# Table steps in VectorE's gaps, retention's state in PSUM, and later column turns in a two-layer hybrid trunk

## The chip, the cores and the metric

The kernel runs on one core of a Trainium2 chip. The metric is the device time of one execution in microseconds (us); each kernel is run several times and the median counts.

## The reference

Two layers of `x <- x + W_out(concat[A(h) * silu(g_A), B(h) * silu(g_B)])` with `h = RMSNorm(x)`, then a last RMSNorm. There are 2048 tokens, 1024 channels, float32.

```
A: 8 heads x 64, softmax over the own chunk of 64 tokens and 8 chunks before it,
   scores * 64**-0.5 + rel_bias[h, clip(distance, -256, 256)]
B: 4 heads x 128, retention in chunks:
   q, k = rotary(q), rotary(k) * 128**-0.5
   o_intra = (q k^T * decay^|i-j|) v          inside a chunk
   o_inter = (q * q_decay) state              state of the chunks before
   state   = state * chunk_decay + (k * k_decay)^T v
   o = rms_norm(o_intra + o_inter)
```

## The kernel before

**Tiles.** Tokens lie in 16 tiles of 128 (`t`) and 4 supertiles of 512 (`n`). A layer is worked in 4 column groups `s`; each group holds two attention heads and one retention head. Per group and supertile, `dense_T` (L736; L719 for the very first) makes q and k for attention and for retention with channels on partitions, and `dense_V` (L755) makes v, the retention v and the gates with tokens on partitions. Every float32 product is made of three float16 products (upper times upper, and both cross terms), so each operand is split into an upper half (ScalarE) and a rest (VectorE). After the four groups `wout` (L1098) multiplies by W_out, adds to x and, in the first layer, makes the next layer's normed columns in `residual`.

**Who sets the order.** The orders on TensorE, ScalarE, VectorE and GpSimd are those in which the Python code issues; the planner leaves them alone. SP, which starts all DMAs, is ordered by hand in the first supertile alone; after that the planner orders its queue by its own estimates. The body is a sequence of rounds of 8 matmuls of 512 columns. `later(k, fn)` puts a step off by k rounds, `pull` brings in background steps (weights for the next group, norms, tables), and `attention` and `retention` of one supertile run under the dense products of the next.

**The first list.** Up to the first `dense_V`, the steps stand in one hand-written list of names that `do` runs in order: `xsq xrs xmul xtr xhi xlo` plus a digit are the steps of a tile's norm (square sum, inverse root, scaling, transposes, upper, rest), `Wsq Wlp Wsc Whi Wlo` and `V...` the steps of a weight section (square sum, cast, scale, upper, rest), `d` the next piece of the first `dense_T`, `t` and `u` the next step of the rotary tables of supertiles 0 and 1, `r` a step of the reversed bias, `g` of the gain, `bs` of the bias scratch, `Tu` and `Vu` the small factors. A table takes 17 steps: one on ScalarE, 13 on VectorE (L93 to L115), the sines on ScalarE (L117, L118), a copy (L120), and 8 stores that SP starts (L125 to L128). The cast in `Vlp2` (L1238) feeds a matmul of ones (L1244) that stands in TensorE's order between two pieces of `d`.

**Retention.** Per tile of 128 tokens, `retention` makes `r1` (the masked products, split into `dT`), then `r2` in PSUM: columns 0 to 127 the output, 128 to 255 the update of the state. One round later `add` (L897, L900 for the first tile) makes `state = update + state` in SBUF; then `upper_of` (L861, ScalarE) and `rest_of` (L865, VectorE) split it into `sh`, which the next tile's `r2` reads; at round 5 ScalarE multiplies the state by the decay in place (L905). `root` and `fin` (L914) finish the output from `r2`. `psR` holds the four PSUM buffers for these.

**Attention's output.** `pv` (L823 to L825) makes `o`; `out_` takes the reciprocal of the sum (L829), multiplies it by the scale `ka` (L830, two tensors of one column) and applies it (L835). The probabilities' rests are made on GpSimd (L813) and turned by a DMA transpose (`pT`).

**Border.** In `wout` of the first layer a tile takes 6 rounds. When its second half is done, SP stores it to `x_d` (L1107) and `residual` sets events at rounds after it: square sum at 2, root at 3. Tiles 5, 6, 7, 9, 10, 11 are turned by TensorE (`on_pe`: `mul` L994 at 5, `turn` L999 at 7, upper 8, rest 9); the others by two DMA transposes from row buffers (`mul` 4, upper 5, rest 6, `transpose_rows` L235, L236 at 7). Tiles 0 to 3 put these rows into slots 2 and 3 of the next layer's weight tiles, in turn. `y_turn` uses the same two lines for W_out's operands (`yhy`, `yly`).

Of the kernel before, what the change touches and what calls it, by code (L numbers as in the profile page):

```python
# [27 lines left out]
def hybrid_trunk(ctx: ExitStack, tc: tile.TileContext, x, pos, gain, gcol, w_in, w_out, rel, fgain,  # L28
# [569 lines left out]
    def later(k, fn):  # L598
        deferred.append([k, fn])
# [181 lines left out]
    def attention(l, s, n, g, st, prev):  # L781
        units = []
        for a in range(4):
            for hx in range(2):
                units.append((a, hx))
        ya = {}

        def qk(a, hx):

            u = St()  # L790
            u.a, u.hx = a, hx
            u.nm = f"{l}_{s}_{n}_{a}_{hx}"
            u.nb = nb = min(5, 4 * n + a + 1)
            u.w = w = nb * P
            u.kts = [(st if t // 4 == n else prev, t % 4) for t in range(4 * n + a + 1 - nb, 4 * n + a + 1)]
            S = psS.tile([P, 1024], F32, tag="S", name=f"S{u.nm}")
            cs = slice(a * P, (a + 1) * P)
            cuts = sorted({0, nb} | {j for j in range(nb) if u.kts[j] == (st, 0) or j == 4})
            for j0, j1 in zip(cuts, cuts[1:]):
                q_, a_ = u.kts[j0]  # L800
                k_ = q_.k[:, hx, a_ * P:(a_ + j1 - j0) * P]
                o = S[:, j0 * P:j1 * P]
                pe.matmul(o, st.q[:, hx, 0, cs], k_, start=True, stop=False)  # L803
                pe.matmul(o, st.q[:, hx, 1, cs], k_, start=False, stop=True)  # L804
            v = b2.tile([P, 640], F32, tag="sc", name=f"sc{u.nm}")[:, 0:w]
            m = b2.tile([P, 1], F32, tag="mq", name=f"mq{u.nm}")
            dve.tensor_tensor_reduce(out=v, in0=S[:, 0:w], in1=g.bias[hx][:, 640 - w:640], scale=1.0, scalar=-3.0e38,  # L807
                                     op0=ALU.add, op1=ALU.max, accum_out=m)
            dve.tensor_scalar(m, m, g.nc[:, 0:1], LN_PSC, op0=ALU.mult, op1=ALU.add)
            act.activation(v, v, AF.Exp, bias=m[:, 0:1], scale=g.c[:, 0:1])  # L810
            pq = b2.tile([P, 1280], F16, tag="pq", name=f"pq{u.nm}")
            act.activation(pq[:, 0:w], v, AF.Copy)  # L812
            pool.tensor_tensor(pq[:, w:2 * w], v, pq[:, 0:w], op=ALU.subtract)  # L813
            u.p = b2.tile([P, 10, P], F16, tag="pT", name=f"pT{u.nm}")[:, 0:2 * nb, :]
            later(1, lambda: sp.dma_start_transpose(out=u.p, in_=pq[:, 0:2 * w]))
            return u

        def pv(u):
            t = 4 * n + u.a
            o = psR.tile([P, 512], F32, tag="small", name=f"o{u.nm}")  # L820
            for b, (q_, a_) in enumerate(u.kts):
                v_ = q_.v[:, a_, u.hx, :]
                pe.matmul(o[:, 0:65], u.p[:, b, :], v_[:, 0:65], start=(b == 0), stop=False)  # L823
                pe.matmul(o[:, 0:64], u.p[:, b, :], v_[:, 65:129], start=False, stop=False)  # L824
                pe.matmul(o[:, 0:65], u.p[:, u.nb + b, :], v_[:, 0:65], start=False, stop=(b == u.nb - 1))  # L825

            def out_():
                rl = b2.tile([P, 1], F32, tag="rl", name=f"rl{u.nm}")
                dve.reciprocal(rl, o[:, 64:65])  # L829
                dve.tensor_tensor(rl, rl, g.ka, op=ALU.mult)  # L830
                if u.hx == 0:
                    ya[u.a] = b2.tile([P, P], F32, tag="ya", name=f"ya{u.nm}")
                y = ya[u.a]
                vs = slice(u.hx * 64, u.hx * 64 + 64)
                dve.scalar_tensor_tensor(out=y[:, vs], in0=o[:, 0:64], scalar=rl[:, 0:1], in1=st.g[u.a][:, vs],  # L835
                                         op0=ALU.mult, op1=ALU.mult)
                if u.hx == 1:
                    sp.dma_start(y_d[t][:, s * P:(s + 1) * P], y)

            later(1, out_)  # L840

        ret = retention(l, s, n, g, st)
        rounds_ret = (5, 10, 10, 14, 14, 18, 18, 23) if (l, s, n) == (0, 0, 0) else [6 * a + b for a in range(4) for b in (0, 5)]
        for i, (a, hx) in enumerate(units):
            flow(1)
            u = qk(a, hx)
            for r in range(3 * i, 3 * i + 3):
                for _ in range(rounds_ret.count(r)):
                    next(ret, None)
                if r % 3 == 2:  # L850
                    pipe.append(lambda u=u: pv(u))
                yield
# [14 lines left out]
    def retention(l, s, n, g, st):  # L867
        for a in range(4):
# [18 lines left out]
            if not last:  # L887
                kh, kl = st.kt[:, a, :], st.kt[:, 4 + a, :]
                products(r2[:, P:2 * P], [(kh, rv[:, 0]), (kh, rv[:, 1]), (kl, rv[:, 0])])
                if t == 0:  # L890
                    ring["state"] = b1.tile([P, P], F32, tag="state", name=f"state{nm}")
                ns = ring["state"]
                sh = ring["halves"] = b1.tile([P, 2, P], F16, tag="sh", name=f"sh{nm}")

                def add(r2=r2, ns=ns, t=t):
                    if t > 0:
                        dve.scalar_tensor_tensor(out=ns, in0=r2[:, P:2 * P], scalar=2.0 ** (-7 - s), in1=ns,  # L897
                                                 op0=ALU.mult, op1=ALU.add)
                    else:
                        dve.tensor_scalar(ns, r2[:, P:2 * P], 2.0 ** (-7 - s), None, op0=ALU.mult)  # L900

                later(1, add)
                later(2, lambda sh=sh, ns=ns: upper_of(sh, ns))
                later(3, lambda sh=sh, ns=ns: rest_of(sh, ns))
                later(5, lambda ns=ns: act.activation(ns, ns, AF.Copy, scale=(1.0 - 2.0 ** (-5 - s)) ** P))  # L905
            ss = b2.tile([P, 1], F32, tag="rss", name=f"rss{nm}")

            def root(ss=ss):
# [71 lines left out]
    def residual(l, t, xt, at, rows, on_pe):  # L980

        hh, hl = (h_[:, :, t % 4 * P:(t % 4 + 1) * P] for h_ in hT_of(l, t // 4))
        nm = f"n{l}_{t}"
        u = St()

        def sq():
            u.ss = squares(xt.rearrange("p (k c) -> p k c", c=P), nm, hh)

        def root():
            u.rs = rms_of(u.ss, gains[l].m, gains[l].e, nm)  # L990

        def mul():
            u.x = xt if on_pe or rows else psS.tile([P, D], F32, tag="S", name=f"xn{nm}")
            dve.scalar_tensor_tensor(out=u.x, in0=xt, scalar=u.rs[:, 0:1], in1=gains[l].b, op0=ALU.mult, op1=ALU.mult)  # L994

        def turn():
            u.p = psS.tile([P, KT, P], F32, tag="S", name=f"pt{nm}")
            for kt in range(KT):
                pe.transpose(u.p[:, kt, :], xt[:, kt * P:(kt + 1) * P], ident)  # L999

        def upper():
            if on_pe:
                act.activation(hh, u.p, AF.Copy)
            else:
                u.rows = rows or row_pair(nm)
                rows_hi(u.rows, u.x)

        def lower():
            if on_pe:
                dve.tensor_tensor(hl, u.p, hh, op=ALU.subtract)  # L1010
            else:
                rows_lo(u.rows, u.x)

        at(2, sq)
        at(3, root)
        if on_pe:
            at(5, mul)
            at(7, turn)
            at(8, upper)
            at(9, lower)  # L1020
        else:
            at(4, mul)
            at(5, upper)
            at(6, lower)
            at(7, lambda: transpose_rows(u.rows, hh, hl))

    def final_half(t, xt, c):

# [30 lines left out]
    def wout(l, go, gc, us, wT=None):  # L1059
# [6 lines left out]
        for r in range(6 * NT):  # L1066
# [32 lines left out]
            if i % 3 == 2:  # L1099
# [4 lines left out]
                if c == 1:  # L1104
                    at = lambda k, fn, r=r: events.setdefault(r + k, []).append(fn)
                    if not end:
                        sp.dma_start(x_d[t], u.x)  # L1107
                        rows = [w_[:, 2 + t % 2].rearrange("p k c -> p (k c)") for w_ in (wT.g.h, wT.g.l)]
                        residual(l + 1, t, u.x, at, rows if t < 4 else None, 4 < t < 12 and t % 4 > 0)
                    elif t + 1 < NT:  # L1110
                        final(t, u.x, at)
            yield
# [238 lines left out]
    def rounds(lists):  # L1351
# [1 line left out]
            do(names)  # L1353
            yield

    do("xsq0 g g xrs0 g Wsq0 Wlp0 Wsc0 xmul0 xtr0 Whi0 xsq1 xhi0 xrs1 xlo0 xmul1 Wlo0 xsq2 d t Wsq1 xrs2 xtr1 t xhi1 Wlp1 xmul2 "
# [3 lines left out]
    g00.vdone = 4  # L1360
    push(rounds(["xhi4 xrs5 xrs6", "xlo4 xmul5 xrs7", "xdma4 xhi5 xmul6 bt", "xlo5 xhi6", "xdma5 xlo6 xmul7", "xdma6 xhi7",
                 "xlo7", "xdma7 bt", "x8 u", "u x8 bt", "u u x8", "u u x8 bt"]), 12)
# [141 lines left out]
```

## Time and profile before

| What | us |
|---|---|
| median of 3 runs | 2089.33 |
| lowest, highest | 2085.60, 2089.53 |
| the profiled execution's own time | 2084.99 |
| its span, first to last instruction | 2083.2 |
| TensorE busy in it | 2008.0 |
| VectorE, ScalarE, GpSimd busy | 1245.1, 1141.9, 679.1 |

Busy times are of one execution, taken by the hardware profiler. PE is TensorE's matmuls, PEld its weight loads, DVE VectorE, ACT ScalarE, POOL GpSimd, SP the engine that starts DMAs. In a row of the timeline stand the start, the duration, engine and line, the operation, what it writes and reads, and in brackets how long the engine sat idle before it and what ended that. The granted clock is the share of full speed at which TensorE was let run.

### The profile page before, as it was taken

The numbers are of one execution on the slowest core, as the hardware profiler recorded it, in microseconds if no ns is written. First come the engines' busy times: TensorE is split into PE (matmuls) and PEld (weight loads), VectorE is DVE, ScalarE is ACT, GpSimd is POOL, SyncE is SP. The second block draws the span as 40 slices with busy tenths as digits, with TensorE's granted clock in tenths as the row PEclk, the third lists the DMA queues.
The fourth block names the chain that finished last, engine by engine and source line by source line (L and its number), as shares of the span: only waits on it lengthen the run. The fifth ranks groups of instructions, "written<-read, shape, count | busy, mean of one in ns | idle before, by whom it ended". The sixth has DMA issues, their size and how long they took to land.

```text
span 2083.2 us, 39398 instructions
## 1 busy us (share of the span) xinstructions
PE 2008.0 (96%) x14014; PEld 1051.6 (50%) x14014; DVE 1245.1 (60%) x3817; ACT 1141.9 (55%) x2530; POOL 679.1 (33%) x701
## 2 busy tenths in 40 slices
PE   6988999999999999998999999999999999999998
PEld 4444555555555555544444555555555555554543
DVE  7776666556556655676653656565655566557643
ACT  7556665456565654554444546554655665446432
POOL 0234343444344434330003343434243334333100
PEclk9999999999999999999999999999999999999999
DMA  8768675547575754799774547555655867548974
GB/s 233 166 152 172 143 164 106 117 112 158 114 185 118 158 141 102 158 227 259 200 188 98 124 102 147 119 124 102 142 119 125 182 145 166 122 102 192 213 197 126
DMA packets 645701, 313.63 MB, mean 151 GB/s; under 512 B 459232, under 2 KB 602080, under 8 KB 645504
## 3 DMA queue, kind: packets, MB, share of 16 engines
q1 hardware_dynamic: 645504, 311.12, 66.0%
q8 instruction: 109, 1.79, 0.4%
q14 instruction: 88, 0.72, 0.1%
HBM read 123.26 MB, written 41.98 MB: 79 GB/s over the span
## 4 chain that ended last, share of the span: by engine, by line
PE 48%; DMA 3%; POOL 1%; issue 1%; DVE 1%; ACT 1%; SPq 0%; POOLq 0%; ACTq 0%; DVEq 0%
PE dT L736 14%; PE dV L755 14%; PE dO L1098 13%; DMA pT<-pq 2%; PE r L857 2%; PE S L804 1%; PE S L803 1%; PE o L823 1%; PE o L824 1%; PE o L825 1%; DMA toep<-rel_d 0%; POOL pq L813 0%; PE ptn L999 0%; DMA stO1m<-in_w_out_dram 0%; ACT sc L810 0%
## 5 line engine op out<-in xcount | busy, mean ns | idle before, releaser
L813 POOL TENSOR_TENSOR pq<-sc,pq 128x640 f16<-128x640 f32 (+4 forms) x256 | 319.9, 1250 | 894.6 <-ACT pq L812 479.7
L810 ACT ACTIVATE sc<-sc,mq,cT 128x640 f32<-128x640 f32 (+4 forms) x256 | 218.5, 853 | 623.8 <-DVE rl L829 324.3
L736 PE MATMUL dT<-hTh,whT 128*128 128x512 f16 x1008 | 350.4, 383 | 5.0 <-DMA hTh<-xa 2.2
L755 PE MATMUL dV<-whV,hTh 128*128 128x512 f16 x1024 | 353.1, 381 | 1.7 <-DVE gt L773 1.3
L755 PE MATMUL dV<-wlV,hTh 128*128 128x512 f16 x1024 | 353.0, 380 | 0.0
L755 PE MATMUL dV<-whV,hTl 128*128 128x512 f16 x1024 | 352.8, 380 | 0.0
L736 PE MATMUL dT<-hTl,whT 128*128 128x512 f16 x1008 | 348.4, 381 | 0.0
L736 PE MATMUL dT<-hTh,wlT 128*128 128x512 f16 x1008 | 348.1, 380 | 0.0
L755 PEld LDWEIGHTS <-hTh 128*128 128x128 f16 x2048 | 196.5, 98 | 217.0 <-DVE gt L773 3.8
L736 PEld LDWEIGHTS <-whT 128*128 128x128 f16 x2016 | 193.1, 98 | 217.8 <-issue 12.9
L807 DVE CUSTOM_DVE_ANT_0 sc<-S,bias 128x640 f32<-128x640 f32 (+4 forms) x256 | 188.4, 736 | 125.3 <-PE S L804 124.6
L1098 PE MATMUL dO<-whO,yhy 128*128 128x512 f16 x512 | 194.6, 380 | 1.0 <-DMA yhy<-hTh 0.8
L1098 PE MATMUL dO<-whO,yly 128*128 128x512 f16 x512 | 194.3, 380 | 1.2 <-DMA yly<-hTl 0.6
L1098 PE MATMUL dO<-wlO,yhy 128*128 128x512 f16 x512 | 194.4, 380 | 0.0
L812 ACT ACTIVATE pq<-sc 128x640 f16<-128x640 f32 (+4 forms) x256 | 171.5, 670 | 8.1
L1098 PEld LDWEIGHTS <-yhy 128*128 128x128 f16 x1024 | 99.8, 98 | 116.1 <-DMA yhy<-hTh 1.3
L755 PEld LDWEIGHTS <-hTl 128*128 128x128 f16 x1024 | 99.2, 98 | 110.8 <-issue 1.7
L736 PEld LDWEIGHTS <-wlT 128*128 128x128 f16 x1008 | 97.5, 98 | 112.9 <-issue 6.2
L823 PE MATMUL o<-v,pT 128*128 128x65 f16 x1120 | 130.5, 194 | 15.6 <-DMA pT<-pq 15.5
L803 PE MATMUL S<-k,q 128*128 128x128 f16 (+3 forms) x592 | 143.6, 269 | 0.0
L823 PEld LDWEIGHTS <-pT 128*128 128x128 f16 x1120 | 106.0, 97 | 53.0 <-DMA pT<-pq 24.4
L804 PE MATMUL S<-k,q 128*128 128x128 f16 (+3 forms) x592 | 131.0, 269 | 0.0
(352 smaller groups left out, 3497.3 us busy)
## 6 DMA issues: line engine op xcount, KB each, us to landing
q<-qq SPq DMA_DIRECT2D x128, 128.0 KB, 2.5
yyy<-y_d SPq DMA_DIRECT2D x32, 512.0 KB, 4.9
stT<-in_w_in_dram SPq DMA_DIRECT2D x27, 512.0 KB, 5.0
stV<-in_w_in_dram SPq DMA_DIRECT2D x26, 512.0 KB, 4.5
k<-kk SPq DMA_DIRECT2D x128, 64.0 KB, 2.0
swp<-rot SPq DMA_DIRECT2D x64, 128.0 KB, 2.7
tabc<-tab SPq DMA_DIRECT2D x32, 256.0 KB, 2.7
tabs<-tab SPq DMA_DIRECT2D x32, 256.0 KB, 3.1
```

Of the source, the lines that this page charges most:

```text
L736: pe.matmul(ps, w_[:, j, kt, :], h_[:, kt, :], start=(m == 0), stop=(m == 23))
L755: pe.matmul(ps, h_[:, kt, a * P:(a + 1) * P], w_[:, kt, :], start=(m == 0), stop=(m == 23))
L803: pe.matmul(o, st.q[:, hx, 0, cs], k_, start=True, stop=False)
L804: pe.matmul(o, st.q[:, hx, 1, cs], k_, start=False, stop=True)
L807: dve.tensor_tensor_reduce(out=v, in0=S[:, 0:w], in1=g.bias[hx][:, 640 - w:640], scale=1.0, scalar=-3.0e38, op0=ALU.add, op1=ALU.max, accu ...
L810: act.activation(v, v, AF.Exp, bias=m[:, 0:1], scale=g.c[:, 0:1])
L812: act.activation(pq[:, 0:w], v, AF.Copy)
L813: pool.tensor_tensor(pq[:, w:2 * w], v, pq[:, 0:w], op=ALU.subtract)
L823: pe.matmul(o[:, 0:65], u.p[:, b, :], v_[:, 0:65], start=(b == 0), stop=False)
L824: pe.matmul(o[:, 0:64], u.p[:, b, :], v_[:, 65:129], start=False, stop=False)
L857: pe.matmul(out_, w_, m_, start=(i == 0), stop=(i + 1 == len(pairs)))
L1098: pe.matmul(ps, h_[:, kt, :], w_[:, kt, :], start=(m == 0), stop=(m == 23))
```

## The change

- The first list is ordered anew. The steps are the same; only their places differ. Four table steps stand right behind the norm of the third tile, the rests of a tile and of a weight swap places in places, and the last table steps stand further back.
- In retention, `add` writes the new state into columns 384 to 511 of `r2` in PSUM, where the upper and the rest are read from; ScalarE's decay goes from there to the state in SBUF, at round 4.
- In `out_`, the multiplication by `ka` takes it as a scalar per partition.
- In `residual`, tiles turned by TensorE have `mul`, `turn`, upper and rest one round later. Tiles 0 to 3 have `mul` at 6, upper at 8, rest at 9 and the transposes at 21, with a slot of its own for each tile. Of the others, tiles 4 and 8 turn at 10 and the last ones at 8.

SP's queue is planned anew with that: each pair of transposes of tiles 0 to 3 stands behind the store of the following tile and behind W_out's next two transposes, and the stores of the first table behind the swap of rq.

```
-                dve.tensor_tensor(rl, rl, g.ka, op=ALU.mult)
+                dve.tensor_scalar(rl, rl, g.ka[:, 0:1], None, op0=ALU.mult)
...
+                new = r2[:, 3 * P:4 * P]
-                def add(r2=r2, ns=ns, t=t):
+                def add(r2=r2, ns=ns, new=new, t=t):
                     if t > 0:
-                        dve.scalar_tensor_tensor(out=ns, in0=r2[:, P:2 * P], scalar=2.0 ** (-7 - s), in1=ns,
+                        dve.scalar_tensor_tensor(out=new, in0=r2[:, P:2 * P], scalar=2.0 ** (-7 - s), in1=ns,
...
-                later(2, lambda sh=sh, ns=ns: upper_of(sh, ns))
-                later(3, lambda sh=sh, ns=ns: rest_of(sh, ns))
-                later(5, lambda ns=ns: act.activation(ns, ns, AF.Copy, scale=(1.0 - 2.0 ** (-5 - s)) ** P))
+                later(2, lambda sh=sh, new=new: upper_of(sh, new))
+                later(3, lambda sh=sh, new=new: rest_of(sh, new))
+                later(4, lambda ns=ns, new=new: act.activation(ns, new, AF.Copy, scale=(1.0 - 2.0 ** (-5 - s)) ** P))
...
         if on_pe:
-            at(5, mul)
-            at(7, turn)
+            at(6, mul)
+            at(8, turn)
+            at(9, upper)
+            at(10, lower)
+        elif rows:
+            at(6, mul)
             at(8, upper)
             at(9, lower)
+            at(26 - 5, lambda: transpose_rows(u.rows, hh, hl))
         else:
             at(4, mul)
             at(5, upper)
             at(6, lower)
-            at(7, lambda: transpose_rows(u.rows, hh, hl))
+            at(8 if t > 8 else 10, lambda: transpose_rows(u.rows, hh, hl))
...
-                        rows = [w_[:, 2 + t % 2].rearrange("p k c -> p (k c)") for w_ in (wT.g.h, wT.g.l)]
-                        residual(l + 1, t, u.x, at, rows if t < 4 else None, 4 < t < 12 and t % 4 > 0)
+                        rows = [w_[:, t].rearrange("p k c -> p (k c)") for w_ in (wT.g.h, wT.g.l)] if t < 4 else None
+                        residual(l + 1, t, u.x, at, rows, 4 < t < 12 and t % 4 > 0)
...
-    do("xsq0 g g xrs0 g Wsq0 Wlp0 Wsc0 xmul0 xtr0 Whi0 xsq1 xhi0 xrs1 xlo0 xmul1 Wlo0 xsq2 d t Wsq1 xrs2 xtr1 t xhi1 Wlp1 xmul2 "
-       "Wsc1 xsq3 Wsq2 xrs3 t xtr2 xlo1 xhi2 d Whi1 t xlo2 Wsq3 xmul3 d r Vsq0 Wlp2 Wlo1 t Wsc2 xtr3 Vsq1 r d xhi3 "
-       "t Vlp0 Whi2 Vsc0 t xlo3 Whi3 bs t d Vhi0 Wlo2 d Vhi1 Wlo3 t d d d Vlo0 t t Vsq2 d t Vlo1 t u Vsq3 t d Vlp2 t d t Tu Vsc2 t xsq4 "
-       "Vhi2 Vhi3 d d Vlo2 Vlo3 xsq5 d Vu d xsq6 xrs4 d Vu xmul4 xsq7 d")
+    do("xsq0 g g xrs0 g Wsq0 Wlp0 Wsc0 xmul0 xtr0 Whi0 xsq1 Wlo0 xhi0 xrs1 xmul1 xlo0 xsq2 d xrs2 t t Wsq1 xtr1 xmul2 Wlp1 t t "
+       "xhi1 Wsc1 xtr2 xlo1 xsq3 xhi2 Wsq2 xrs3 d Whi1 xlo2 xmul3 Wlo1 Wsq3 d Wlp2 xtr3 Vsq0 Wsc2 d xhi3 Vsq1 xlo3 Whi2 Vlp0 t t "
+       "Whi3 Wlo2 d Vsc0 Wlo3 r t Vhi0 d t Vhi1 d r bs d Vlo0 t d Vsq2 d t Vlo1 Vsq3 d Vlp2 t d t Vsc2 Vhi2 t d Vhi3 t Tu t xsq4 "
+       "t d Vlo2 t u Vlo3 d t xsq5 d Vu xsq6 xrs4 d Vu xmul4 xsq7 d")
```

More of the change, by code (lines that the diff above doesn't have):

```diff
@@ L893, in retention @@
                 sh = ring["halves"] = b1.tile([P, 2, P], F16, tag="sh", name=f"sh{nm}")
-                def add(r2=r2, ns=ns, t=t):
+                new = r2[:, 3 * P:4 * P]
+                def add(r2=r2, ns=ns, new=new, t=t):
                     if t > 0:
-                        dve.scalar_tensor_tensor(out=ns, in0=r2[:, P:2 * P], scalar=2.0 ** (-7 - s), in1=ns,
+                        dve.scalar_tensor_tensor(out=new, in0=r2[:, P:2 * P], scalar=2.0 ** (-7 - s), in1=ns,
                                                  op0=ALU.mult, op1=ALU.add)
                     else:
-                        dve.tensor_scalar(ns, r2[:, P:2 * P], 2.0 ** (-7 - s), None, op0=ALU.mult)
+                        dve.tensor_scalar(new, r2[:, P:2 * P], 2.0 ** (-7 - s), None, op0=ALU.mult)
                 later(1, add)
-                later(2, lambda sh=sh, ns=ns: upper_of(sh, ns))
-                later(3, lambda sh=sh, ns=ns: rest_of(sh, ns))
-                later(5, lambda ns=ns: act.activation(ns, ns, AF.Copy, scale=(1.0 - 2.0 ** (-5 - s)) ** P))
+                later(2, lambda sh=sh, new=new: upper_of(sh, new))
+                later(3, lambda sh=sh, new=new: rest_of(sh, new))
+                later(4, lambda ns=ns, new=new: act.activation(ns, new, AF.Copy, scale=(1.0 - 2.0 ** (-5 - s)) ** P))
             ss = b2.tile([P, 1], F32, tag="rss", name=f"rss{nm}")
```

## The prediction

> **What bounds the kernel now.** I read the page's span and busy times first, then busy time by stage, then who waited for whom on TensorE, then the timeline around each long wait, and last the order of instructions of both programs.
>
> ```profile
> span 2083.2 us, 39398 instructions
> PE 2008.0 (96%) x14014; PEld 1051.6 (50%) x14014; DVE 1245.1 (60%) x3817; ACT 1141.9 (55%) x2530; POOL 679.1 (33%) x701
> ```
>
> TensorE is busy for 2008.0 of 2083.2 us and the change leaves its matmuls as they are, so only its 75 us of idleness, and its slow clock, can be won. The stages say where these lie; the columns are the stage, its length, busy us (and instructions) of PE, PE's weight loads, DVE, ACT and POOL, then the granted clock, the DMA share and GB/s:
>
> ```profile
> 0.00:50.00 50.00, 31.68 (x296) 22.90 (x297) 35.43 (x103) 35.61 (x68) 4.88 (x18) 0.97 0.83 236
> 50.00:100.00 50.00, 46.96 (x241) 21.78 (x239) 35.30 (x77) 28.93 (x58) 13.65 (x18) 1.00 0.68 162
> 100.00:300.00 200.00, 178.11 (x1265) 92.99 (x1263) 134.17 (x397) 121.59 (x268) 78.84 (x76) 0.95 0.75 160
> 300.00:870.00 570.00, 567.10 (x4222) 303.03 (x4221) 339.14 (x1137) 324.09 (x761) 221.48 (x221) 1.00 0.60 131
> 870.00:1000.00 130.00, 118.67 (x758) 59.76 (x757) 87.29 (x235) 71.30 (x135) 24.52 (x24) 0.99 1.04 244
> 1000.00:2060.00 1060.00, 1049.25 (x7169) 543.95 (x7167) 606.09 (x1862) 557.10 (x1237) 333.41 (x342) 1.00 0.64 145
> ```
>
> The reader is to see that 300 to 870 and 1000 to 2060 are matmul from end to end (2.9 and 10.8 us idle). VectorE time saved there is worth nothing. The change can act in three places: the first list (18.3 us idle before 50), the stretch to 300 (3.0 and 21.9 us), and the border between the layers (11.3 us).
>
> **First list.** The change moves steps, and removes none. TensorE's last stall in it, and what follows, are these rows of the timeline and one of a finer table of stages:
>
> ```profile
> 37.91 0.87 DVE L93 SCALAR_TENSOR_TENSOR wk<-wk,wk 128x256 f32<-128x256 f32 x2
> 39.31 0.42 DVE L93 SCALAR_TENSOR_TENSOR wk<-wk,wk 128x256 f32<-128x256 f32 x1
> 40.83 0.29 DVE L113 TENSOR_SCALAR wk<-wk 128x256 f32<-128x256 f32 x1
> 41.15 0.42 ACT L117 ACTIVATE wk<-wk 128x256 f32<-128x256 f32 x1 [3.58 <-DVE wk L113]
> 41.16 0.43 DVE L115 SCALAR_TENSOR_TENSOR wk<-wk 128x256 f32<-128x256 f32 x1
> 41.50 0.17 DVE L1238 CAST mbV<-m1V 128x2 bf16<-128x2 f32 x1
> 41.72 0.16 PE L1244 MATMUL ms<-mbV,ones 128*128 128x2 bf16 x1 [2.54 <-DVE mbV L1238]
> 41.74 0.38 PE L736 MATMUL dT<-hTh,wlT 128*128 128x512 f16 x1
> 43.03 0.59 PE L736 MATMUL dT<-hTh,wlT 128*128 128x512 f16 x1
> 55.71 0.28 ACT L763 ACTIVATE v<-dV 128x128 f16<-128x128 f32 x1 [1.88 <-PE dV L755]
> ```
> ```profile
> 40.00:50.00 10.00, 8.29 (x32) 3.49 (x32) 5.67 (x17) 8.58 (x25) 0.63 (x2) 0.83 0.60 160
> ```
>
> The cast (step Vlp2) stands on VectorE behind 14 table steps in the old list and behind 10 in the new one. The four that pass behind it cost 2 x 0.42 + 0.29 + 0.43 = 1.56 us. Four of the ten now run early, in gaps in which VectorE waited for ScalarE; I put 0.6 us on that, an estimate of one and a half such steps that no longer stand in the way. So the stall of 2.54 us falls to about 0.4, and 2.2 us come back. After the stall TensorE ran at half clock: 0.83 over 10 us is 3.4 us at half speed, 1.7 us of work lost. If that goes with the stall, the first dense_V can start 3.9 us earlier.
>
> What is late next is ScalarE. Its 3.58 us of idleness before the table's sine are not removed: in the new list it idles about as long for the last weight scale, then has the same work left, with the sines behind Vhi3 instead of ahead of xsq4. The norms of tiles 4 to 7 behind that work, which the next dense_T needs, gain only where ScalarE itself waited for dense_V: 1.88 us before L763. So this term is **-1.9 us**, with bounds 0 (VectorE's norm chain holds everything) and -3.9. On SP's queue the table stores now stand behind the swap of rq and wait for the later sines; the rotation that needs them feeds retention alone, whose first dT is finished only at 94.5 (its row stands below), and the 40 us until then cover it. Without that cover it would cost what the stores are late, by my estimate the 1.56 us of table steps that moved.
>
> [...]
>
> **Retention and the attention scale, 100 to 300 us.** These rows show VectorE held while GpSimd works, and a TensorE wait behind it:
>
> ```profile
> 107.14 1.32 POOL L679 TENSOR_TENSOR rot<-rot,swp 128x512 f32<-128x512 f32 x1
> 107.26 1.34 DVE L865 SCALAR_TENSOR_TENSOR sh<-sh,state 128x128 f16<-128x128 f16 x1
> 108.66 0.27 PE L857 MATMUL r<-sh,rot 128*128 128x128 f16 x1 [4.12 <-DVE sh L865]
> 129.10 0.92 DVE L830 TENSOR_TENSOR rl<-rl,kaV 128x1 f32<-128x1 f32 x1
> 132.94 0.22 PE L857 MATMUL r<-sh,rot 128*128 128x128 f16 x1 [0.70 <-DVE sh L865]
> ```
>
> Then one line each for four operations (min/median/max in ns), and the busy time of lines 830 and 865 between 100 and 300 us:
>
> ```profile
> L865 DVE SCALAR_TENSOR_TENSOR sh<-sh,state x120: 276/284/1452, 107.3 to 1945.7; 128x128 f16<-128x128 f16 x120
> L865 DVE SCALAR_TENSOR_TENSOR dT<-dT,r x128: 269/277/289, 94.5 to 1947.1; 128x128 f16<-128x128 f16 x128
> L830 DVE TENSOR_TENSOR rl<-rl,kaV x256: 158/159/1333, 93.3 to 1960.6; 128x1 f32<-128x1 f32 x128
> L809 DVE TENSOR_SCALAR mq<-mq,ncT x256: 212/214/216, 75.5 to 1948.2; 128x1 f32<-128x1 f32 x128
> ```
> ```profile
> 100.00:300.00 200.00, 8.06 (x27) 0.95 0.75 160
> 100.00:300.00 200.00, 10.01 (x28) 0.95 0.75 160
> ```
>
> With the state in PSUM, rest_of(sh) has the form of dT's (one SBUF tensor, one PSUM), and that form never took over 289 ns: 1.34 becomes 0.28, and 1.06 of the 4.12 us goes. The scale `rl` takes the form of L809, which is 55 ns dearer (214 against 159) and never held (216 at most). The second wait for sh, 0.70 us, comes 3.8 us behind the `rl` at 129.10, which was held for 0.92 - 0.16 = 0.76 us in the same queue, and goes. That is 1.06 + 0.7, **-1.8 us**. Bounds: all holds of this stretch at best, (8.06 - 27 x 0.159) + (10.01 - 28 x 0.28) = 5.9 us; at worst the holds pass to the next two-tensor operation and only 27 x 0.055 = 1.5 us of dearer scales stay. Over the rest of the span the same two edits save more VectorE time, beside matmuls that never stop: nothing.
>
> [...]
>
> **Border between the layers.** Waits of TensorE between 870 and 1000 us, and the longest chain in it:
>
> ```profile
> PE o L823 <- DMA pT<-pq: 5.5, 4, 2.1
> PE dO L1098 <- DMA yhy<-hTh: 0.8, 1, 0.8
> PE dO L1098 <- DMA yly<-hTl: 0.6, 1, 0.6
> PE dO L1098 <- DMA yly<-hTh: 0.6, 1, 0.6
> ```
> ```profile
> 964.79 3.89 SPq L236 DMA_TRANSPOSE hTl<-rln  x1
> 970.13 0.53 SPq L1107 DMA_DIRECT2D x_d<-hTh  x1
> 973.43 1.29 DVE L994 SCALAR_TENSOR_TENSOR hTh<-hTh,rsn,gb 128x1024 f32<-128x1024 f32 x1 [4.86 <-DMA x_d<-hTh]
> 974.77 1.88 PE L999 MATMUL ptn<-ident,hTh 128*128 128x128 f32 x8 [2.06 <-DVE ymy L954]
> ```
>
> Tile 5's `mul` overwrites what SP still stores to x_d5, so VectorE stood 4.86 us and TensorE's transposes 2.06. One round later for mul and turn lets TensorE do 8 more matmuls first, which at (43.03 - 41.74) / 6 = 0.215 us from start to start are 1.7 us. Of the transposes of tiles 0 to 3, each pair now stands on SP behind one or two of the attention's and W_out's transposes, which should land earlier (5.5 + 2.0 us of waits). But exactly as many issues stand ahead of x_d5 as before, and at 1.04 the DMA engines are full. What TensorE wins before 962 it can lose again at tile 5's turn. I keep 1.5 us of it, an estimate of a fifth of 7.5. Term: **-3.2 us**; bounds -9.5 (all of 7.5 and 2.06) and +3.9 (a slow pair, as at 964.79, now in front of a transpose that TensorE waits for).
>
> The other edits (the last tiles one round later, own slots for four tiles) change waits that TensorE does not have: nothing, with a bound of 1 us to either side.
>
> **Sum.** -1.9 - 1.8 - 3.2 = -6.9 us against the profiled execution, whose own time was 2084.99 (span 2083.2 and 1.79 around it): 2078.1. That execution lies 4.3 under the median of three, 2089.33 (2085.60 to 2089.53), so I set the same difference on the median: **2082.4 us**. A measurement tells about 0.2%, 4.2 us, from no change.
>
> **Rivals.**
> 1. *Absorbed.* The norm chain on VectorE holds the start of the next dense_T, and the full SP queue holds the border; left are 1.06 + 1.7 = 2.8 us: 2086.5, no change. For: the 1.04 DMA share, and TensorE's idle 3.0 us in 50 to 100. Against: ScalarE did wait for dense_V.
> 2. *Slower: the PSUM buffer of retention comes free later.* Its last reader is now ScalarE's decay of the state, in ScalarE's queue behind exponentials, instead of VectorE's `fin`; the matmul that reuses the buffer waits.
>
> ```profile
> 110.16 0.29 ACT L905 ACTIVATE state<-state 128x128 f32<-128x128 f32 x1
> 110.74 0.34 DVE L914 SCALAR_TENSOR_TENSOR yr<-r,rss,gt 128x128 f32<-128x128 f32 x1
> ```
>
> Here the decay, one tick later than in the change, started ahead of `fin`. There are 120 decays; 0.1 us of wait for each is 12 us: 2082.4 + 12 = 2094.4. It decides from (6.9 + 4.2) / 120 = 0.09 us each.
> 3. *More.* The border's waits go entirely and the clock stays up: -3.9 - 1.8 - 9.5 = -15.2: 2074.1.
>
> **Numbers.** Forecast 0.46, absorbed 0.28, slower 0.14, more 0.12. Faster is 0.46 + 0.12 = 0.58, the same 0.28, slower 0.14. The range runs from just under rival 3 to rival 2: 2073 to 2094.
>
> **What would show it.** Right: no wait for mbV over 1 us, L763 without idleness before 55 us, no sh above 300 ns, `rl` near 214 and never held, the stall at L999 under 1 us. Wrong: dense_T of the second supertile starting no earlier than before; a TensorE wait released by ScalarE's decay; waits for pT and yhy in the border that sum to 7.5 us again.

## Result: 0.1 to 0.2% slower, where 0.3% faster was forecast

The changed kernel took 2092.41 us (median of 9 runs, 2088.66 to 2095.11) against 2086.03 us for the kernel before in the same session (9 runs, 2082.95 to 2092.67). The ratio on record is 1.0022, 95% interval 1.0011 to 1.0032, or 4.6 us more; the two medians by themselves lie 6.4 us apart. In a second session the ratio was 1.0011 (0.9998 to 1.0025). The forecast was 2082.4, which is 6.9 us under the first three runs of before (2089.33).

The page of the changed kernel, its span and its busy times:

```profile
span 2091.1 us, 39382 instructions
PE 2010.8 (96%) x14014; PEld 1052.7 (50%) x14014; DVE 1178.3 (56%) x3817; ACT 1144.8 (55%) x2530; POOL 677.4 (32%) x701
```

The profiled execution's own time was 2092.88 us. VectorE lost 66.8 us of busy time (1245.1 to 1178.3) and the span grew by 7.9 us. Busy times by stage, columns as in the prediction:

```profile
0.00:50.00 50.00, 35.23 (x312) 25.41 (x313) 35.90 (x102) 35.43 (x67) 4.75 (x18) 1.00 0.81 230
50.00:100.00 50.00, 45.11 (x230) 20.57 (x229) 36.69 (x82) 29.57 (x59) 16.38 (x19) 1.00 0.70 171
100.00:300.00 200.00, 174.92 (x1249) 91.06 (x1248) 130.16 (x393) 121.22 (x267) 77.61 (x74) 0.96 0.74 158
300.00:870.00 570.00, 565.48 (x4215) 302.24 (x4213) 310.26 (x1133) 322.50 (x755) 219.98 (x221) 1.00 0.59 130
870.00:1000.00 130.00, 119.84 (x760) 59.97 (x758) 88.48 (x236) 73.85 (x142) 24.40 (x25) 0.97 1.07 246
1000.00:2060.00 1060.00, 1046.14 (x7150) 542.70 (x7149) 566.31 (x1856) 556.62 (x1235) 331.34 (x341) 0.99 0.62 145
```

The reader is to see three things. The first 50 us are better: 14.8 us idle on TensorE instead of 18.3, at full clock. The two stretches that were matmul from end to end are worse: 4.5 us idle instead of 2.9 between 300 and 870, 13.9 instead of 10.8 after 1000, although VectorE has 69 us less to do in these two. So a cost arose in the place that the prediction set aside. And the stretch ahead of them is worse too: from 50 to 300 us TensorE idles 30.0 us instead of 24.9, where the prediction had put a gain. The table by stage under "Side by side" shows that this loss is there with the state in SBUF as well.

**First list.** The rows of the timeline and of the finer stage that answer to those of before, and a new wait behind them:

```profile
40.03 0.16 PE L1251 MATMUL ms<-mbV,ones 128*128 128x2 bf16 x1
53.92 0.27 ACT L763 ACTIVATE v<-dV 128x128 f16<-128x128 f32 x1
65.03 0.39 PE L755 MATMUL dV<-whV,hTh 128*128 128x512 f16 x1 [2.18 <-DVE gt L773]
```
```profile
40.00:50.00 10.00, 9.97 (x48) 4.54 (x48) 5.26 (x16) 8.29 (x24) 0.63 (x2) 1.00 0.60 161
```

The stall of 2.54 us for mbV is gone, the clock is 1.00 where it was 0.83 (0.50 from 44 to 46 us), and ScalarE no longer waits ahead of L763. At 65 us TensorE then stands 2.18 us for an eviction (VectorE's copy of finished sums out of PSUM).

**Retention.** VectorE's holds by GpSimd are gone, as worked out. Before, 50 of the 120 rests of sh and 60 of the 256 `rl` took over 1.2 times their median, up to 1.45 and 1.33 us, each of them beside an operation of GpSimd. Now none does, though 61 and 69 run beside one; the longest take 289 and 216 ns:

```profile
L865 DVE SCALAR_TENSOR_TENSOR sh<-sh,r x120: 270/280/289, 106.4 to 1953.4; 128x128 f16<-128x128 f16 x120
L830 DVE TENSOR_SCALAR rl<-rl,kaV x256: 212/214/216, 92.1 to 1968.5; 128x1 f32<-128x1 f32 x128
```

The waits that the prediction counted on did not all go with the holds. TensorE's waits for sh from 100 to 300 us (total, times, longest), before and after, and the second of them, which was to go and stayed:

```profile
PE r L857 <- DVE sh L865: 4.8, 2, 4.1
```
```profile
PE r L857 <- DVE sh L865: 4.0, 2, 3.3
```
```profile
130.18 0.29 DVE L769 SCALAR_TENSOR_TENSOR v<-dV,v 128x128 f16<-128x128 f32 x1 [0.43 <-ACT rv L765]
132.44 0.22 PE L857 MATMUL r<-sh,rot 128*128 128x128 f16 x1 [0.77 <-DVE sh L865]
```

`rl` takes 0.21 us there, but VectorE then waits 0.43 us for ScalarE in the same queue.

**Border.** TensorE's waits from 870 to 1000 us (total, times, longest). The stall of 2.06 us at the transposes is gone, and one of 3.7 us for `yly`, the low half of W_out's operand for the tile that TensorE is at, stands in its place:

```profile
PE o L823 <- DMA pT<-pq: 4.6, 3, 2.6
PE dO L1105 <- DMA yly<-hTl: 3.7, 1, 3.7
```

**What is new.** The final step of retention (`fin`, line 914 before, 916 after) waits for ScalarE's decay of the state. The group of the changed kernel (total busy, mean ns, idle time of VectorE before it and what ended it; before, that was 26.9 us, nearly all behind GpSimd):

```profile
L916 DVE SCALAR_TENSOR_TENSOR yr<-r,rss,gt 128x128 f32<-128x128 f32 x128 | 44.4, 347 | 51.4 <-POOL rss L912 44.7 <-ACT state L907 4.6 <-issue 1.3
```

The view puts most of the rise down to GpSimd, and that is misleading, as one `fin` shows:

```profile
516.50 0.54 POOL L912 TENSOR_TENSOR rss<-rss,mhalf 128x1 f32<-128x1 f32 x1
517.46 0.27 ACT L907 ACTIVATE state<-r 128x128 f32<-128x128 f32 x1
517.83 0.35 DVE L916 SCALAR_TENSOR_TENSOR yr<-r,rss,gt 128x128 f32<-128x128 f32 x1 [2.75 <-POOL rss L912]
```

GpSimd was done at 517.04 and the decay at 517.73; `fin` started at 517.83. Taken one by one in the trace, 22 of the `fin` start about 0.1 us after the end of a decay, with GpSimd done before it, and 27.6 of the 51.4 us stand before these.

### The profile page after: what moved, and what is told of

The parts are those of the page before. It is cut to its first block, busy times and chain, and to the rows that moved or that the text cites. A ratio compares the mean times of both kernels' runs of the same rounds, so it can differ in the third digit from the quotient of the medians.

```text
span 2091.1 us, 39382 instructions
## 1 busy us (share of the span) xinstructions
PE 2010.8 (96%) x14014; PEld 1052.7 (50%) x14014; DVE 1178.3 (56%) x3817; ACT 1144.8 (55%) x2530; POOL 677.4 (32%) x701
## 4 chain that ended last, share of the span: by engine, by line
PE 49%; DMA 3%; ACT 2%; DVE 1%; issue 1%; SPq 0%; POOLq 0%; ACTq 0%; DVEq 0%
PE dT L736 15%; PE dV L755 14%; PE dO L1105 13%; DMA pT<-pq 2%; PE r L857 2%; PE S L804 1%; PE S L803 1%; PE o L823 1%; PE o L824 1%; PE o L825 1%; ACT stO1m L312 0%; DMA yly<-hTl 0%; ACT sc L810 0%; DMA stO1m<-in_w_out_dram 0%; DVE sc L807 0%
## 5 line engine op out<-in xcount | busy, mean ns | idle before, releaser
L823 PE MATMUL o<-v,pT 128*128 128x65 f16 x1120 | 130.7, 194 | 18.6 <-DMA pT<-pq 18.5
```

## Experiments

Each kernel differs from the changed one (or, where said, from the one before) by the edit shown. Ratios are to the kernel before on the same chip, 9 to 12 runs each (6 for the first), with 95% intervals.

### One part undone at a time

```
e1_no_state:   state added into SBUF (out=ns), decay in place at later(5)
e1_no_rl:      dve.tensor_tensor(rl, rl, g.ka, op=ALU.mult)
e1_no_border:  mul, turn, transpose_rows and the rows' slots as before
e1_no_list:    the first list as before
```

> The changed kernel with retention's state as before: written to SBUF by VectorE, decayed in place by ScalarE at later(5). Theory S (the state in PSUM costs: the decay's place on ScalarE makes the final step of retention and its store late, SP's queue and then the pT transposes follow): the 4.6 us of loss go, 2086 to 2088, and the waits of TensorE for pT at the group changes fall from 18.5 to about 15.5 us in sum. Theory F (the loss is made at the group changes by the phase of the DMA queue, whatever part shifts it): within 2 us of the changed kernel. The prediction's own term says it gets slower by about 1 us (the hold of 1.3 us on VectorE comes back before 300 us).

> The changed kernel with the scale rl as a product of two tensors again. Theory R (55 ns dearer scales, 256 of them, 14 us of VectorE, delay VectorE's part of the chain at each group change): 1 to 3 us faster than the changed kernel. Theories S and F: within 1.5 us of it.

> The changed kernel with the border between the layers as before (mul, turn and row transposes in their old rounds, shared slots for tiles 0 to 3). Theory B (the later turn and transposes cost): 2 to 4 us faster, the wait of 3.68 us for yly at 964 us is gone. From the comparison of the two traces, which puts the border at about -0.2 us net, theories S, R and F expect within 1.5 us of the changed kernel.

> The changed kernel with the first list as before. Theory L (the new list pays 3.35 us at 50 us and loses it again by 300 us through its new wait of 2.2 us at 62.9): within 1.5 us of the changed kernel. If the list's gain stays, it is 2 to 3 us slower; if the list as a whole costs, 2 to 4 us faster. The wait for mbV of 2.5 us is back in its trace, and the wait of 2.2 us for the eviction of dense_V at 62.9 is gone.

Measured: without the state in PSUM 0.9971 (0.9960 to 0.9982), 2080.48 us. Without the new scale 1.0013 (1.0000 to 1.0025), without the border 1.0019 (1.0007 to 1.0031), without the list 1.0013 (1.0003 to 1.0023). Only the state turns the sign, so of the four theories S alone explains the loss; that the other parts cost or save 1 or 2 us is not excluded, as the changed kernel itself lies between 1.0011 and 1.0022. S was too small (it gave 2086 to 2088), and the place that it names, the decay's in ScalarE's queue, is tested below. The trace without the state in PSUM at the last group of layer 0, about 880 us, beside the changed kernel's, shows a first wait. First the changed kernel:

```profile
880.60 0.26 ACT L861 ACTIVATE dT<-r 128x128 f16<-128x128 f32 x1
880.76 1.14 ACT L333 ACTIVATE whO<-stO,o_s 128x1024 f16<-128x1024 f32 x1
881.28 0.40 DVE L773 SCALAR_TENSOR_TENSOR gt<-gt,dV 128x256 f32<-128x256 f32 x1
881.80 0.27 ACT L907 ACTIVATE state<-r 128x128 f32<-128x128 f32 x1
882.16 0.35 DVE L916 SCALAR_TENSOR_TENSOR yr<-r,rss,gt 128x128 f32<-128x128 f32 x1 [0.47 <-issue]
882.43 0.28 DVE L865 SCALAR_TENSOR_TENSOR dT<-dT,r 128x128 f16<-128x128 f16 x1
882.76 0.23 PE L857 MATMUL r<-rv,dT 128*128 128x128 f16 x1 [1.39 <-DVE dT L865]
```

Then the one with the state in SBUF:

```profile
879.03 0.40 DVE L773 SCALAR_TENSOR_TENSOR gt<-gt,dV 128x256 f32<-128x256 f32 x1
879.36 0.34 DVE L914 SCALAR_TENSOR_TENSOR yr<-r,rss,gt 128x128 f32<-128x128 f32 x1
879.62 0.27 DVE L865 SCALAR_TENSOR_TENSOR dT<-dT,r 128x128 f16<-128x128 f16 x1
879.95 0.23 PE L857 MATMUL r<-rv,dT 128*128 128x128 f16 x1 [0.93 <-DVE dT L865]
882.58 0.29 ACT L905 ACTIVATE state<-state 128x128 f32<-128x128 f32 x1
```

With the state in SBUF, `fin` starts 0.33 us after the eviction `gt` and the lower half of dT stands right behind it. In the changed kernel `fin` starts 0.88 us after it, 0.09 after the end of the decay, and the decay itself stood behind a weight piece of 1.14 us in ScalarE's queue. `fin` uses nothing that the decay makes. In the instruction order of the compiled program 120 of the 128 `fin` wait for ScalarE, and none with the state in SBUF: both read the same PSUM buffer r2, and here the program puts accesses of two engines to one buffer in order. The traces agree: in the changed kernel all 120 `fin` of tiles that have a decay start at least 0.09 us after its end, with the state in SBUF 1 of 120 does. The price is not paid by `fin`, whose result is not urgent, but by what is queued behind it on VectorE: the lower half of dT, for which TensorE waits 1.39 us instead of 0.93.

Over the whole execution this wait tells the kernels apart. TensorE's waits for dT (total, times, longest) before, in the changed kernel, with the state in SBUF, and with the decay at later(5) in PSUM, the first run of the next group:

```profile
PE r L857 <- DVE dT L865: 8.7, 11, 2.3
```
```profile
PE r L857 <- DVE dT L865: 11.0, 13, 2.3
```
```profile
PE r L857 <- DVE dT L865: 8.6, 12, 2.3
```
```profile
PE r L857 <- DVE dT L865: 8.2, 11, 2.3
```

In the six traces with the state in PSUM and its decay at later(4) the total is 11.0 to 12.2 us, in the thirteen others 8.2 to 9.3. This is about 3 us of the cost, by an estimate from the two means (11.7 and 8.7).

### Which of the state's waits

```
e2_decay5:            later(5, <decay>)   # state in PSUM
e2_sbuf_decay4:       later(4, <decay>)   # state in SBUF
e2_sbuf_square_first: state in SBUF; later(2, <square>) ahead of later(2, <upper half>)
e2_only_state:        before + the state in PSUM, decay at later(4)
```

> The changed kernel with the decay of the state one tick later, later(5) as before; the state stays in PSUM. In the program's order the final step of retention on VectorE then no longer waits for the decay, but the rest of sh still waits for the square of the retention's output on ScalarE, and the matmul of o that takes over the PSUM buffer still waits for the decay. Theory Fin (VectorE's wait for the decay costs): most of the 10 us between the changed kernel (ratio 1.0022) and the one without the PSUM state (0.9971) come back, ratio 0.999 or less. Theory Square (the wait of sh for the square costs): ratio stays at 1.001 to 1.002. Theory Buffer (rival 2 of the prediction: the PSUM buffer comes free later): slower than the changed kernel, ratio over 1.003.

> The changed kernel with the state in SBUF, but its decay at later(4) as in the changed one. If the place of the decay in ScalarE's queue costs by itself, ratio 1.000 or more; theories Fin, Square and Buffer all say no shared PSUM buffer, no cost: 0.996 to 0.998, as without the PSUM state.

> The state in SBUF, everything else as changed, but ScalarE does the square of retention's output ahead of the upper half of the state, so that the rest of sh on VectorE waits for the square too, as it does with the state in PSUM. Theory Square: the cost comes back without any PSUM state, ratio 1.000 to 1.002. Theories Fin and Buffer: 0.996 to 0.998.

> The kernel before with the state in PSUM and its decay at later(4) as the only edit. If the cost of this part stands by itself: ratio 1.004 to 1.006 (10 us), and the rest of the change is worth -6 us. If it only costs together with the new list or the border: 0.999 to 1.002.

Measured: 1.0003 (0.9991 to 1.0014), 0.9976 (0.9964 to 0.9987), 0.9979 (0.9963 to 0.9995) and 1.0029 (1.0016 to 1.0041). The decay's place on ScalarE costs nothing by itself that the timing shows, and neither does the wait of sh for the square: theory Square falls. The state alone costs 6 us in the kernel before (0.0029 x 2085). With later(5) `fin` comes ahead of the decay again and its idle time falls from 51.4 to 32.4 us:

```profile
L916 DVE SCALAR_TENSOR_TENSOR yr<-r,rss,gt 128x128 f32<-128x128 f32 x128 | 44.4, 347 | 32.4 <-POOL rss L912 32.1 <-issue 0.3
```

Part of the loss comes back (1.0003 against 1.0022 and 1.0011), less than theory Fin wanted. One new wait is theory Buffer's, the prediction's second rival, now in TensorE's waits of this run:

```profile
PE r L857 <- ACT state L907: 2.7, 3, 1.1
```

### The decay early, and the rest of the change without the state

```
e3_decay2:             later(2, <decay>)   # right behind the upper half
e3_no_state_no_list:   scale and border alone
e3_no_state_no_border: scale and list alone
e3_no_state_no_rl:     list and border alone
```

> The changed kernel with the decay of the state at later(2), right behind the upper half and ahead of the square; the state stays in PSUM. In the program's order nothing on VectorE or TensorE waits for the decay any more: neither the final step (120 such waits in the changed kernel, none with later(5)), nor the matmuls of o and r that take over the buffer (90 in the changed kernel, 100 with later(5)). Only the rest of sh waits for the square, which cost nothing with the state in SBUF. Theory Waits (the cost is Fin and Buffer together): ratio 0.996 to 0.998, as without the PSUM state. Theory Access (reading or writing the state in PSUM costs by itself, or ScalarE's wait for its own upper half): 1.000 or more, as with later(5) at 1.0003.

> The state in SBUF and the first list as before: of the change only the scale rl and the border are left. Prediction's term for the list, 1.9 us: ratio 0.998 against the 0.9971 with the list. If the list's gain is lost again by 300 us: 0.997. If the list carries the whole gain: 1.000.

> The state in SBUF and the border as before: of the change only the scale rl and the first list are left. Prediction's term for the border, 3.2 us: ratio 0.9986. If the border is worth nothing (its waits for yly replace those it removes, as the two first traces show): 0.997. If the border carries the whole gain: 1.000.

> The state in SBUF and the scale rl as a product of two tensors: of the change only the list and the border are left. Prediction: the scale is worth 0.7 us, ratio 0.9974. If the holds of rl by GpSimd (up to 1.3 us each) delay VectorE's chain at each group change and so TensorE: 0.9985 to 1.000.

Measured: 0.9999 (0.9990 to 1.0009), 0.9985 (0.9974 to 0.9997), 0.9981 (0.9970 to 0.9992) and 0.9988 (0.9973 to 1.0002). With later(2) neither `fin` nor a matmul that takes over the buffer waits for the decay, `fin`'s idle time is 32.1 us, and still the kernel is no faster than before. TensorE's waits for dT are down to 8.3 us in its trace, so something else took the place of that wait. The three pairs lie between 0.9981 and 0.9988. Beside the three timings of all three parts together (0.9971, and 0.9989 and 0.9986 below) no part's own worth can be told from zero in time; each interval is about 2.5 us to either side.

What took its place is seen on SyncE. Its queue is filled by a scheduler from modelled times, not by hand, and the order of the compiled program shows it changed with the decay at later(4), later(5) and later(2) in PSUM, and unchanged with the decay at later(4) in SBUF: in the border the load of tile 3 stands ahead of a store and an attention transpose. SyncE's timeline with later(5):

```profile
882.16 0.32 SPq L935 DMA_DIRECT2D yyy<-y_d  x1
882.59 0.91 SPq L838 DMA_DIRECT2D y_d<-ya  x1
883.60 3.00 SPq L815 DMA_TRANSPOSE pT<-pq  x1
```

TensorE's wait for that transpose was 4.4 us in this run and 4.3 with later(2), against 1.9 to 2.8 with the state in SBUF. The changed kernel has the same order, but its wait there is only 1.3 and 0.9 us in its two traces. So this wait is a price of the runs with the decay moved, and is not shown to be part of the changed kernel's loss.

### SyncE's order put back

```
+ with tc.issue_after(<attention transpose>):   # for the load of tile 3 in layer 0, decay at later(2) or later(5);
      sp.dma_start(u.y, y_d[t])                 # with later(2) also for five transposes of k
```

> The state in PSUM with its decay at later(2), as in the run before, and SyncE's queue in the order that it has with the state in SBUF (one load still stands three places later): the load of tile 3 in the border and five transposes of k are held behind the attention's transpose. Theory Order (SyncE's other order is the rest of the cost): ratio 0.997 to 0.998, and the wait for pT at about 889 us falls from 4.3 to about 2 us. Theory Access (the state in PSUM costs by itself): stays at 0.9995 to 1.0005.

> The state in PSUM with its decay at later(5), and SyncE's queue in exactly the order that it has with the state in SBUF. What is left is the buffer that waits for the decay (2.7 us of TensorE's waits in the first such run). Theory Order: 0.998 to 0.999, the wait at about 889 us at about 2 us. Theory Access: 1.000 as before.

> The changed kernel with the state in SBUF once more (two comment lines aside the same as the first run of it), as the reference on the same chip: 0.996 to 0.998.

Measured: 1.0000 (0.9985 to 1.0015), 0.9994 (0.9984 to 1.0005) and 0.9989 (0.9975 to 1.0002). The longest wait fell as theory Order said, and the times did not: it wanted 0.997 to 0.999. The third run is the changed kernel with the state in SBUF once more, also above its 0.996 to 0.998. TensorE's waits for pT from 870 to 1000 us, with later(5), first with SyncE's own order, then with the one put back:

```profile
PE o L823 <- DMA pT<-pq: 8.0, 3, 4.4
```
```profile
PE o L823 <- DMA pT<-pq: 5.3, 3, 2.4
```

In time the step from 1.0003 to 0.9994 is within the intervals, and 1.0000 with later(2) speaks for no gain at all. On this chip the kernel with the state in SBUF lies 0.0005 and 0.0011 under the two, which can't be told from nothing either. So the traces show the waits; that the accesses to PSUM cost nothing by themselves is not shown.

### Side by side

> The changed kernel unaltered, for a comparison on one chip with the next run. If the state in PSUM is what turned the gain into a loss: ratio 1.001 to 1.003.

> The changed kernel with retention's state in SBUF and its decay at later(5), as before. If the rest of the change is worth what the prediction gave to the list, the scale and the border (5 to 6 us): ratio 0.997 to 0.998, 8 to 10 us under the changed kernel on the same chip.

Measured: the changed kernel 1.0011 (0.9998 to 1.0025), 2087.19 us; with the state in SBUF 0.9986 (0.9971 to 1.0001), 2081.17 us, against 2083.71 before. The state costs 6.0 us on one chip, 2087.19 - 2081.17, less than the 8 to 10 expected (and 0.9986 is short of the 0.997 to 0.998); the two intervals just overlap here, and were far apart in the first comparison (1.0022 and 0.9971). The kernel with the state in SBUF is under both others in all three of its timings (0.9971, 0.9989, 0.9986; mean 0.9982, 3.8 us under before).

Aligned at the same dense matmuls, TensorE's gain (-) or loss (+) against the one profiled execution of before, in us by stage, mean of the traces of each kernel, tells where:

```
stage up to (us)                     50    300    850   1000   1690   1930    sum
changed (2 traces)                 -3.5   +3.9   +2.8   -1.7   -1.0   +4.8   +5.3
state in SBUF (3 traces)           -3.6   +4.1   -0.4   -2.5   -1.5   +0.4   -3.4
state in SBUF, list as before (1)  -0.1   +2.6   +1.1   -3.5   -1.1   +1.1    0.0
PSUM, later(5), later(2) (1 each)  -3.2   +1.8   +1.5   +2.1   -3.4   +0.7   -0.6
```

These are few traces, and the two of the changed kernel lie 5.2 us apart in sum (+7.9 and +2.7), so a difference of 1 or 2 us in a stage says little. Of the 8.7 us between the first two rows, 7.5 arise between 300 and 850 and after 1690, in TensorE's waits for retention's dT and attention's pT around the changes of group. The waits for pT are the part left open: 16.3 and 18.5 us in the changed kernel's traces, 13.0 to 16.7 in the three of the second row. The last row shows the trade of the moved decay: the loss after 1690 is nearly gone, and the border loses 2.1 us where the changed kernel gains 1.7.

## Why the prediction was wrong, step by step

- **First list, -1.9 us, bounds 0 and -3.9.** The mechanism was right. The stall for mbV is 0.2 us, the clock is full, L763 has no wait, and the first dense_V starts 3.37 us earlier (46.96 us, it was 50.33; 3.9 was worked out). With the state in SBUF, the trace without the list gains 0.1 there and the three with it 3.6. From there to 300 us they lose 4.1, the one without it 2.6, so that some 2 us are left of it, near the forecast; the timing doesn't resolve this. The wait of 2.18 us at 65 us may be a price of the list: it stands in 14 of the 15 traces with the new list, as 1.6 us in two with the old one, and not at all in the two others (before, and the changed kernel with the old list). Why all these kernels lose after 50 us stays open.
- **Retention and scale, -1.8 us, bounds -5.9 and +1.5.** This is the step that failed. The durations were right (280 for 284 ns, at most 289; `rl` 214), and VectorE became freer by 67 us. But the term counted durations and not the waits that the shared buffer adds. In its own stretch the waits for sh fell by 0.8 us (4.8 to 4.0) instead of 1.8: the second one stayed, as VectorE waited for ScalarE in the time that `rl` saved. Over the whole kernel the state's part measured +6.0 us side by side and +6 alone, outside both bounds. The sentence that left all of it "beside matmuls that never stop: nothing" is where it went: at each change of group TensorE does wait for VectorE, and there an operation behind a false wait costs: about 3 us of the loss is in the waits for dT. The rest, mostly waits for pT by the traces, is not traced to its cause.
- **Rival 2, +12 us, given 0.14.** It named the instruction, the decay as last reader of r2, and its result of 2094.4 was near, but by luck: it looked for the price at the matmul that reuses the buffer, 0.1 us for every tile. Such waits are seen only with later(5), 2.7 us in 3. The price at later(4) was paid behind VectorE's own `fin`, in dT, at a few tiles. The row shown there, a decay that started ahead of `fin`, was read as harmless; it is the order that is now forced. The prediction's test, "a TensorE wait released by ScalarE's decay", missed for the same reason: ScalarE releases VectorE, and VectorE TensorE.
- **Border, -3.2 us, bounds -9.5 and +3.9.** Too large. From 850 to 1000 us the kernels with it gain 1.7 and 2.5 us, and the one without it but with the state in SBUF 1.4 (one trace). Tile 5's stall of 2.06 us went as said, but its successor is close to the one named under "Wrong", where yhy stands for yly: 4.6 + 3.7 = 8.3 us of waits for pT and yly stand where 7.5 stood.
- **Scale `rl`.** 55 ns dearer and never held, as forecast; its worth is inside the noise (0.9988 without, 0.9982 with, the state in SBUF in both).

What would have shown the failure blind is the list of waits in the instruction order of the changed program: 120 new waits of `fin` for ScalarE.

## What to carry to other kernels

When a value moves into a buffer that other steps use, count the buffer's readers and writers on each engine: accesses that share no data were put in order here too (120 of the 128 `fin` behind ScalarE), and the wait was paid by what was queued behind it (TensorE's waits for dT: 11.0 us, 8.7 before). VectorE, 56% busy, still stood on the path at changes of group, so an edit on such an engine is costed at those places, not at the average. Look also at queues that a scheduler orders by modelled times: an edit on two engines moved a load on a third.

## What was not expected of the hardware

In the changed kernel a wait of TensorE of 1.90 us was followed by a stretch with the clock at 0.71 (stages of 5 us):

```profile
1708.57 0.20 PE L823 MATMUL o<-v,pT 128*128 128x65 f16 x1 [1.90 <-DMA pT<-pq]
```
```profile
1710.00:1715.00 5.00, 5.00 (x20) 2.06 (x19) 1.94 (x11) 3.31 (x12) 1.69 (x3) 0.71 0.58 134
```

At 0.71 over 5 us, 1.45 us of work were lost on top of the 1.90, by an estimate from the clock (0.29 x 5). The stall of 2.18 us at 65 us was not followed by one: the clock from 50 to 100 us is 1.00.

ScalarE was faster here from PSUM than from SBUF: the upper half of the state takes 258 ns (it was 293), the decay 274 (293). VectorE's addition of the state, written to PSUM, takes 290 instead of 282 ns. All of these are medians.
